# A gated short-convolution layer in fp32: the gate's sums over partitions as two fp32r products, and the output in transfers of 1024 columns

## The chip, the core and the metric

The kernel runs on one core of a Trainium2 chip. The metric is the device time of one execution in microseconds. The engines are TensorE (PE: matmuls, with its weight loads shown as PEld), VectorE (DVE), ScalarE (ACT), GpSimd (POOL) and SyncE (SP), whose queue issues nearly all transfers here. A transfer runs on the core's DMA engines.

## What is computed

One layer over 256 tokens of width D = 2048, with E = 4096 channels in the mixer, all in fp32. Cut to what the one layer of this case does:

```python
def rmsnorm(x, g):
    y = x * lax.rsqrt(jnp.mean(x * x, axis=-1, keepdims=True) + EPS)
    return y * g

def short_conv_mixer(h, w_in, conv_w, w_out):
    proj = jnp.einsum('bsd,de->bse', h, w_in)          # 2048 -> 4 x 4096
    b_gate, c_gate, v, g = jnp.split(proj, 4, axis=-1)
    u = causal_depthwise_conv(c_gate * v, conv_w)      # width 3
    y = b_gate * u * jax.nn.silu(g)
    return jnp.einsum('bse,ed->bsd', y, w_out)         # 4096 -> 2048

mod = jnp.einsum('bd,df->bf', jax.nn.silu(c), ada_w) + ada_b   # 2048 -> 3 x 2048
shift, scale, gate = jnp.split(mod, 3, axis=-1)
h = rmsnorm(x, norm_g) * (1.0 + scale[:, None, :]) + shift[:, None, :]
x = x + gate[:, None, :] * short_conv_mixer(h, sc_w_in, sc_conv_w, sc_w_out)
out = rmsnorm(x, final_g)
```

## The kernel before

**Exact products.** A fp32 matrix is split into two fp32r parts, `hi` (a cast on ScalarE, L337) and `lo` (the fp32 remainder, a subtraction on VectorE, L338). A product of two matrices is then three fp32r matmuls: hi by hi, hi by lo, lo by hi. The weights are loaded raw from memory in tiles of 128 x 2048 (`raw_s`, `raw`, `raw_o`), by SP's queue, with three buffers each for `raw`, `hi` and `lo`. A `raw` buffer is loaded again when VectorE has made its `lo`; a `hi` buffer is cast again when TensorE has used it. TensorE takes 48 matmuls of 256 columns from each tile of the input projection.

**Stages.** First the norm, the first parts of shift and scale and the features `hT`. Then the input projection in two forms: `parts` (tile `mm_s`, up to about 383 us) goes over two channel groups at a time and over parts of the depth, as the shift and scale for more of the depth become known; its sums are kept in `acc` tiles between parts. Then whole products (`mm_b`, up to about 732 us). Last the output projection (`mm_o`), for the four column groups `dc` of 512 columns and the two halves `t` of the tokens.

**The banks in `parts`.** Three PSUM banks of the tag `mm` take turns. When TensorE has finished one, `keep` drains it, on ScalarE by a copy (L497) or on VectorE by an add into `acc` (L499). The bank's next user may be seeded: ScalarE copies an `acc` into it (L511) before TensorE adds to it. VectorE and ScalarE also do `mixed` here: gating, convolution (L408 to L412) and the split of the result `y` (L417, L418).

**The gate.** `gate` is a vector of 2048, needed on all 128 partitions. It is made in four pieces of 512 columns. `ada_w`'s part for it comes in 32 loads (`at_g`, four buffers of the tag `at`), each used by two steps on VectorE, which multiply by `silu_c` and add into `gacc` (two buffers). After 16 steps `gacc` holds, on each partition, a part of the sum. One fp32 matmul with a matrix of ones sums over the partitions and spreads the sum to all of them (L604), and VectorE adds the bias (L605). The text calls the four pieces gate 0 to gate 3.

**The end.** `po[t]` for the last column group already holds x, and the gate is multiplied into the weights, so `po` is the result before the norm. `gated` squares and sums it on ScalarE (L726), and `finish(t)` takes the root and the reciprocal `fs`, multiplies four column pieces of 512 by `fs`, two on VectorE and two on ScalarE, and sends each piece by a transfer of its own on SP's queue (L685). The first half's `finish` runs while TensorE still does the last products of the second half (`late`).

**Order.** In the first stage the instructions of each engine stand in the order of the program. After it a scheduler orders each engine's queue by priorities and its own estimate of times; `later(GIVE)` puts the gate's steps behind other work by 300 places. Each engine then works through its queue in that order, with semaphores for what it needs of others. Buffers of a tag go to whoever is next when one is free.

Of the kernel before, what the change touches and what calls it, by code (L numbers as in the profile page):

```python
# [13 lines left out]
P = 128  # L14
# [114 lines left out]
def short_conv_layer(ctx: ExitStack, tc: tile.TileContext, x, c, norm_g, ada_w, ada_b, w_in, conv_w, w_out, final_g, out):  # L129
# [95 lines left out]

    ident = const.tile([P, P], F32, tag="ident", name="ident")
    make_identity(nc, ident)
    ones = const.tile([P, P], F32, tag="ones", name="ones")
    nc.vector.memset(ones, 1.0)
    eps_t = const.tile([P, 1], F32, tag="eps", name="eps_t")  # L230
    nc.vector.memset(eps_t, EPS)
# [359 lines left out]
    def gate_sums(dc, j, at3):  # L591
        nc.sync.dma_start(at3, adas[:, j : j + 2, 2, dc * 512 : (dc + 1) * 512])
        if j == 0:
            gacc[0] = adap.tile([P, 512], F32, tag="gv", name="gacc")
        ga = gacc[0]
        for i in range(2):
            s = silu_c[:, j + i : j + i + 1]
            if j + i == 0:
                nc.vector.tensor_scalar_mul(ga, at3[:, i, :], s)
            else:  # L600
                nc.vector.scalar_tensor_tensor(out=ga, in0=at3[:, i, :], scalar=s, in1=ga, op0=ALU.mult, op1=ALU.add)
        if j + 2 == KT:
            ps = psum.tile([P, 512], F32, tag="sm", name="ps_gate", bufs=2)
            nc.tensor.matmul(ps, ones, ga, start=True, stop=True)  # L604
            nc.vector.tensor_tensor(out=gate(dc), in0=ps, in1=gate(dc), op=ALU.add)  # L605

    KP = 8
# [63 lines left out]
    def finish(t):  # L671

        fs = const.tile([P, 1], F32, tag="fs", name="fs", bufs=2)
        nc.scalar.activation(fs, fsq[:, t, 3:4], AF.Sqrt, bias=part_sum[:, t : t + 1])
        nc.vector.reciprocal(fs, fs)
        for c0, n, vector in ((0, 512, True), (512, 512, False), (1536, 512, True), (1024, 512, False)):
            dd = slice(c0, c0 + n)
            r = big[:, t, dd]
            if c0 == 1536:
                nc.vector.scalar_tensor_tensor(out=r, in0=po[t], scalar=fs, in1=fg[:, dd], op0=ALU.mult, op1=ALU.mult)  # L680
            elif vector:
                nc.vector.tensor_scalar_mul(r, r, fs)
            else:
                nc.scalar.activation(r, r, AF.Copy, scale=fs)
            nc.sync.dma_start(out[t * P : (t + 1) * P, dd], r)  # L685

    for dc in range(4):
        dcs = slice(dc * 512, (dc + 1) * 512)

        both = [psum.tile([P, TT, 512], F32, tag="mm", name="mm_o") for _ in range(1 + (dc == 3))]  # L690
        po = [both[-t][:, t] for t in range(TT)]
        n_ep = NCT // EP
        late = []
        if dc == 3:

            for t in range(TT):
                nc.scalar.copy(po[t], big[:, t, dcs])
        for ep in range(n_ep):

            first = dc == 0 and ep == 0  # L700
            raw = wpool.tile([P, SLOT], F32, tag="raw" if first else "lo", name="raw_o", bufs=3)
            nc.sync.dma_start(
                raw.rearrange("p (k f) -> p k f", k=EP),
                w_out[0, ep * EP * P : (ep + 1) * EP * P, dcs].rearrange("(k p) f -> p k f", p=P),
            )
            if dc == 3:

                raw3 = raw.rearrange("p (k f) -> p k f", k=EP)
                nc.vector.tensor_tensor(
                    out=raw3, in0=raw3, in1=gate(dc).unsqueeze(1).to_broadcast([P, EP, 512]), op=ALU.mult  # L710
                )
            hi, lo = split(raw, SLOT, "raw")
            out_mm(po[0], 0, ep, hi, lo)
            if dc == 3 and ep >= n_ep - LATE:
                late.append((ep, hi, lo))
            else:
                out_mm(po[1], 1, ep, hi, lo)

        def gated(t, bank, c0, n):

            cs = slice(dc * 512 + c0, dc * 512 + c0 + n)
            r = big[:, t, cs]
            p0 = (dc % 2) * 1024 + t * 512 + c0
            pr = big[:, 3, p0 : p0 + n]
            if dc == 3:
                nc.scalar.activation(pr, bank, AF.Square, scale=D**-0.5, accum_out=fsq[:, t, dc : dc + 1])  # L726
                return
            nc.vector.tensor_tensor(out=pr, in0=bank, in1=gate(dc)[:, c0 : c0 + n], op=ALU.mult)
            nc.vector.tensor_tensor(out=r, in0=r, in1=pr, op=ALU.add)
            nc.scalar.activation(pr, r, AF.Square, scale=D**-0.5, accum_out=fsq[:, t, dc : dc + 1])  # L730
            nc.vector.tensor_tensor(out=r, in0=r, in1=fg[:, cs], op=ALU.mult)
            if dc == 2:
                ps = part_sum[:, t : t + 1]
                nc.vector.reduce_sum(ps, fsq[:, t, 0:3], axis=mybir.AxisListType.X)
                nc.vector.tensor_scalar_add(ps, ps, EPS)

        gated(0, po[0], 0, 512)
        if dc == 3:
            finish(0)
        for ep, hi, lo in late:  # L740
            out_mm(po[1], 1, ep, hi, lo)
        gated(1, po[1], 0, 512)
    finish(1)


# [22 lines left out]
```

## Time and profile before

| | before |
|---|---|
| median of 3 runs | 916.65 us (916.56 to 916.69) |
| profiled execution | 916.12 us, span 914.3 us |
| granted TensorE clock | 0.997 of full speed |
| TensorE busy | 900.3 us (98%) |
| VectorE busy | 627.2 us (69%) |
| ScalarE busy | 449.7 us (49%) |
| DMA traffic | 227.64 MB, 249 GB/s over the span |

Times in the traces count from the start of the profiled execution's span. A row of the timeline gives start and duration in us, engine, line, operation, tiles and shape, and in brackets how long the engine had been idle before and what ended that. A row of the chain gives start, duration, engine, tile and line, and how many instructions were merged. A row for transfers gives the number, the size of one and the median time from issue to landing in us.

### The profile page before, as it was taken

The numbers are of one execution on the slowest core, as the hardware profiler recorded it, in microseconds if no ns is written. First come the engines' busy times: TensorE is split into PE (matmuls) and PEld (weight loads), VectorE is DVE, ScalarE is ACT, GpSimd is POOL, SyncE is SP. The second block draws the span as 40 slices with busy tenths as digits, with TensorE's granted clock in tenths as the row PEclk, the third lists the DMA queues.
The fourth block names the chain that finished last, engine by engine and source line by source line (L and its number), as shares of the span: only waits on it lengthen the run. The fifth ranks groups of instructions, "written<-read, shape, count | busy, mean of one in ns | idle before, by whom it ended". The sixth has DMA issues, their size and how long they took to land.

```text
span 914.3 us, 16328 instructions
## 1 busy us (share of the span) xinstructions
PE 900.3 (98%) x7111; PEld 866.4 (95%) x7111; DVE 627.2 (69%) x601; ACT 449.7 (49%) x423; POOL 0.7 (0%) x6
## 2 busy tenths in 40 slices
PE   7999999999999999999999999999999999999996
PEld 7899999999999999999999999999999988888885
DVE  4888989999986899985555455545455544555882
ACT  6678876554545745543334443334333333443333
POOL 0000000000000000000000000000000000000000
PEclk9999999999999999999999999999999999999998
DMA  9999999999997569867666666566666496565542
GB/s 302 366 384 377 327 348 357 338 360 328 346 366 270 186 231 328 270 217 229 199 186 188 196 201 200 184 189 195 202 188 196 139 352 205 200 205 188 185 139 92
DMA packets 147367, 227.64 MB, mean 249 GB/s; under 512 B 5424, under 2 KB 103904, under 8 KB 146912
## 3 DMA queue, kind: packets, MB, share of 16 engines
q1 hardware_dynamic: 147056, 226.51, 73.7%
q8 instruction: 55, 0.90, 0.4%
q14 instruction: 16, 0.13, 0.0%
q10 hardware_dynamic: 240, 0.09, 0.0%
HBM read 224.49 MB, written 2.10 MB: 248 GB/s over the span
## 4 chain that ended last, share of the span: by engine, by line
PE 95%; DMA 3%; DVE 1%; ACT 1%; SPq 0%; issue 0%; ACTq 0%; DVEq 0%
PE mm_b L465 38%; PE mm_s L465 37%; PE mm_o L666 6%; PE mm_o L667 6%; PE mm_o L665 6%; DMA raw_s<-in_sc_w_in_dram 1%; DMA at<-in_ada_w_dram 1%; DMA x<-in_x_dram 1%; DVE gv L363 1%; PE ps_gate L604 0%; PE tp_g L454 0%; ACT hi L337 0%; SPq L220 0%; DVE lo L338 0%; PE sum L349 0%; SPq L203 0%
## 5 line engine op out<-in xcount | busy, mean ns | idle before, releaser
L465 PE MATMUL mm_b<-hT,hi 128*128 128x256 f32 x2048 | 348.8, 276 | 0.0
L465 PE MATMUL mm_s<-hT,hi 128*128 128x256 f32 x2048 | 337.0, 277 | 1.6 <-ACT hT L327 1.0
L465 PEld LDWEIGHTS mm_b<-hT,hi 128*128 128x128 f32 x2048 | 308.3, 188 | 0.2 <-issue 0.2
L465 PEld LDWEIGHTS mm_s<-hT,hi 128*128 128x128 f32 x2048 | 299.3, 188 | 2.8 <-ACT hT L327 1.2
L465 PE MATMUL mm_b<-hT,lo 128*128 128x256 f32 x1024 | 282.6, 276 | 0.0
L465 PE MATMUL mm_s<-hT,lo 128*128 128x256 f32 x1024 | 262.1, 276 | 0.0
L338 DVE TENSOR_TENSOR lo<-raw,hi 128x2048 fp32r<-128x2048 f32 x64 | 146.7, 2292 | 128.8 <-ACT hi L337 128.7
L337 ACT CAST hi<-raw 128x2048 fp32r<-128x2048 f32 x64 | 122.4, 1913 | 197.2 <-PE mm_b L465 149.9
L465 PEld LDWEIGHTS mm_b<-hT,lo 128*128 128x128 f32 x1024 | 192.2, 188 | 0.2 <-issue 0.2
L465 PEld LDWEIGHTS mm_s<-hT,lo 128*128 128x128 f32 x1024 | 182.8, 188 | 0.0
L337 ACT CAST hi<-raw_s 128x2048 fp32r<-128x2048 f32 (+1 forms) x64 | 121.4, 1901 | 99.5 <-PE mm_s L465 84.5
L338 DVE TENSOR_TENSOR lo<-raw_s,hi 128x2048 fp32r<-128x2048 f32 (+1 forms) x64 | 145.5, 2273 | 22.5 <-ACT hi L337 21.3
L338 DVE TENSOR_TENSOR lo<-raw_o,hi 128x2048 fp32r<-128x2048 f32 x32 | 73.3, 2291 | 64.5 <-ACT hi L337 64.5
L337 ACT CAST hi<-raw_o 128x2048 fp32r<-128x2048 f32 x32 | 61.0, 1907 | 107.2 <-PE mm_o L667 85.1
L666 PE MATMUL mm_o<-lo,y 128*128 128x512 f32 x256 | 99.7, 391 | 0.0
L665 PE MATMUL mm_o<-hi,y 128*128 128x512 f32 x256 | 99.3, 389 | 0.0
L667 PE MATMUL mm_o<-hi,y 128*128 128x512 f32 x256 | 99.3, 389 | 0.0
L447 DVE SCALAR_TENSOR_TENSOR gv<-at,silu_c,gv 128x512 f32<-128x512 f32 x105 | 78.6, 749 | 2.6 <-DMA at<-in_ada_w_dram 0.8
L666 PEld LDWEIGHTS mm_o<-lo,y 128*128 128x128 f32 x256 | 48.1, 188 | 10.2 <-issue 0.2
L667 PEld LDWEIGHTS mm_o<-hi,y 128*128 128x128 f32 x256 | 48.0, 188 | 10.1 <-issue 0.2
L665 PEld LDWEIGHTS mm_o<-hi,y 128*128 128x128 f32 x256 | 48.0, 188 | 10.0
L497 ACT COPY acc<-mm_s 128x1024 f32<-128x1024 f32 x43 | 43.4, 1018 | 22.2 <-PE mm_s L465 22.0
(102 smaller groups left out, 382.0 us busy)
## 6 DMA issues: line engine op xcount, KB each, us to landing
raw<-in_sc_w_in_dram SPq DMA_DIRECT2D x64, 1024.0 KB, 5.6
raw_s<-in_sc_w_in_dram SPq DMA_DIRECT2D x63, 1024.0 KB, 7.6
raw_o<-in_sc_w_out_dram SPq DMA_DIRECT2D x32, 1024.0 KB, 5.2
at<-in_ada_w_dram SPq DMA_DIRECT2D x114, 256.0 KB, 7.1
at_g<-in_ada_w_dram SPq DMA_DIRECT2D x32, 512.0 KB, 7.5
at<-in_ada_w_dram SPq DMA_DIRECT2D x6, 512.0 KB, 9.0
x<-in_x_dram SPq DMA_DIRECT2D x4, 512.0 KB, 6.7
big<-in_x_dram SPq DMA_DIRECT2D x2, 1024.0 KB, 8.0
```

The costliest lines, as they stand in the source:

```text
L337: nc.scalar.copy(hi[:, :n], raw[:, :n])
L338: nc.vector.tensor_tensor(out=lo[:, :n], in0=raw[:, :n], in1=hi[:, :n].bitcast(F32), op=ALU.subtract)
L363: nc.vector.scalar_tensor_tensor(out=gv0, in0=first_ada[k], scalar=c_k, in1=gv0, op0=ALU.mult, op1=ALU.add)
L447: nc.vector.scalar_tensor_tensor(out=gv, in0=at4[:, i], scalar=c_k, in1=gv, op0=ALU.mult, op1=ALU.add)
L465: mm = last_mm[0] = nc.tensor.matmul(dst, w, h[:, k], start=begins and left, stop=ends, skip_group_check=True)
L497: nc.scalar.copy(acc[ch, q], bank)
L665: nc.tensor.matmul(po, yh, hi[:, o], start=opens, stop=False, skip_group_check=True)
L666: nc.tensor.matmul(po, yh, lo[:, o], start=False, stop=False, skip_group_check=True)
L667: nc.tensor.matmul(po, yl, hi[:, o], start=False, stop=ct == NCT - 1, skip_group_check=True)
```

## The change

Two edits. The gate's `gacc` is split into two fp32r parts in one tile `gate_s` (a buffer of the tag `at`, as the loads `at_g` use), by a cast on ScalarE and a subtraction on VectorE, and two fp32r matmuls with the ones replace the fp32 one. The ones are exact in fp32r. At the end, the squaring moves from `gated` into `finish`, and `finish` sends 1024 columns in one transfer when both of their pieces are done; ScalarE's pieces are written ahead of VectorE's.

```diff
-    ones = const.tile([P, P], F32, tag="ones", name="ones")
+    ones_e = const.tile([P, P], F32R, tag="ones", name="ones")
+    ones = ones_e.bitcast(F32)
...
         if j + 2 == KT:
             ps = psum.tile([P, 512], F32, tag="sm", name="ps_gate", bufs=2)
-            nc.tensor.matmul(ps, ones, ga, start=True, stop=True)
+            parts = adap.tile([P, 2, 512], F32R, tag="at", name="gate_s", bufs=4)
+            nc.scalar.copy(parts[:, 0], ga)
+            nc.vector.tensor_tensor(out=parts[:, 1], in0=ga, in1=parts[:, 0].bitcast(F32), op=ALU.subtract)
+            for i in range(2):
+                nc.tensor.matmul(ps, ones_e, parts[:, i], start=i == 0, stop=i == 1)
             nc.vector.tensor_tensor(out=gate(dc), in0=ps, in1=gate(dc), op=ALU.add)
...
     def finish(t):
         fs = const.tile([P, 1], F32, tag="fs", name="fs", bufs=2)
+        r = big[:, t]
+        pr = big[:, 3, 1024 + t * 512 : 1536 + t * 512]
+        nc.scalar.activation(pr, po[t], AF.Square, scale=D**-0.5, accum_out=fsq[:, t, 3:4])
         nc.scalar.activation(fs, fsq[:, t, 3:4], AF.Sqrt, bias=part_sum[:, t : t + 1])
         nc.vector.reciprocal(fs, fs)
-        for c0, n, vector in ((0, 512, True), (512, 512, False), (1536, 512, True), (1024, 512, False)):
-            dd = slice(c0, c0 + n)
-            r = big[:, t, dd]
-            if c0 == 1536:
-                nc.vector.scalar_tensor_tensor(out=r, in0=po[t], scalar=fs, in1=fg[:, dd], op0=ALU.mult, op1=ALU.mult)
-            elif vector:
-                nc.vector.tensor_scalar_mul(r, r, fs)
-            else:
-                nc.scalar.activation(r, r, AF.Copy, scale=fs)
-            nc.sync.dma_start(out[t * P : (t + 1) * P, dd], r)
+        nc.scalar.activation(r[:, 512:1024], r[:, 512:1024], AF.Copy, scale=fs)
+        nc.vector.tensor_scalar_mul(r[:, 0:512], r[:, 0:512], fs)
+        nc.sync.dma_start(out[t * P : (t + 1) * P, 0:1024], r[:, 0:1024])
+        nc.scalar.activation(r[:, 1024:1536], r[:, 1024:1536], AF.Copy, scale=fs)
+        nc.vector.scalar_tensor_tensor(
+            out=r[:, 1536:D], in0=po[t], scalar=fs, in1=fg[:, 1536:D], op0=ALU.mult, op1=ALU.mult
+        )
+        nc.sync.dma_start(out[t * P : (t + 1) * P, 1024:D], r[:, 1024:D])
```

The edit to the gate also moves instructions between about 250 and 430 us, because the scheduler decides anew. TensorE's order keeps its places: the products of gates 0 and 1 stand next to each other between the same `mm_s` products as before (four rows of one matmul now, two before), those of gate 2 in `mm_b`, those of gate 3 in `mm_o`. Three places of other engines follow; the order has no times in it. In the rows of the change lines are numbered one to five higher (L338 is L339, L499 is L500, L601 is L602).

VectorE, at the tile subtractions (`lo_3495`, `lo_3549`) that stand at 285.06 and 290.50 us in the trace of before. Before:

```order
L338 TENSOR_TENSOR lo_3495<-raw_s_3492,hi_3494 128x2048
L338 TENSOR_TENSOR lo_3549<-raw_s_3546,hi_3548 128x2048
L546 TENSOR_TENSOR acc01_373<-acc01_373,acc02_480 128x512 x2
L499 TENSOR_TENSOR acc12_482<-mm_s_3324,acc12_482 128x1024
L409 SCALAR_TENSOR_TENSOR acc02_480<-acc01_373,cw_128,acc02_480 128x255 x2
```

And in the change:

```order
L339 TENSOR_TENSOR lo_3495<-raw_s_3492,hi_3494 128x2048
L607 TENSOR_TENSOR gate_s_6368<-gacc_5550,gate_s_6368 128x512
L600 TENSOR_SCALAR gacc_6488<-at_g_6486,silu_c_129 128x512
L602 SCALAR_TENSOR_TENSOR gacc_6488<-at_g_6486,silu_c_129,gacc_6488 128x512
L602 SCALAR_TENSOR_TENSOR gacc_6488<-at_g_6601,silu_c_129,gacc_6488 128x512 x2
L339 TENSOR_TENSOR lo_3549<-raw_s_3546,hi_3548 128x2048
L547 TENSOR_TENSOR acc01_373<-acc01_373,acc02_480 128x512 x2
L602 SCALAR_TENSOR_TENSOR gacc_6488<-at_g_6721,silu_c_129,gacc_6488 128x512
L500 TENSOR_TENSOR acc12_482<-mm_s_3324,acc12_482 128x1024
```

The subtraction of gate 1 and the first five steps of gate 2 (`gacc_6488`) now stand here; before, gate 2 began about 30 us later.

VectorE again, from the subtraction of `lo_3773` (307.12 us before) to the add that drains the bank `mm_s_3658` (317.10 us before). Before:

```order
L338 TENSOR_TENSOR lo_3773<-raw_s_3770,hi_3772 128x2048
L499 TENSOR_TENSOR acc13_547<-mm_s_3491,acc13_547 128x1024
L338 TENSOR_TENSOR lo_3832<-raw_s_3829,hi_3831 128x2048
L550 TENSOR_TENSOR acc03_545<-acc03_545,acc00_615 128x512 x2
L499 TENSOR_TENSOR acc10_617<-mm_s_3658,acc10_617 128x1024
```

And in the change:

```order
L339 TENSOR_TENSOR lo_3773<-raw_s_3770,hi_3772 128x2048
L413 SCALAR_TENSOR_TENSOR acc12_482<-acc11_412,cw_128,acc12_482 128x254 x2
L602 SCALAR_TENSOR_TENSOR gacc_6488<-at_g_6952,silu_c_129,gacc_6488 128x512
L413 SCALAR_TENSOR_TENSOR acc12_482<-acc11_412,cw_128,acc12_482 128x254
L500 TENSOR_TENSOR acc13_547<-mm_s_3491,acc13_547 128x1024
L339 TENSOR_TENSOR lo_3832<-raw_s_3829,hi_3831 128x2048
L602 SCALAR_TENSOR_TENSOR gacc_6488<-at_g_6952,silu_c_129,gacc_6488 128x512
L551 TENSOR_TENSOR acc03_545<-acc03_545,acc00_615 128x512 x2
L500 TENSOR_TENSOR acc10_617<-mm_s_3658,acc10_617 128x1024
```

Between `lo_3549` and this last add the change has six steps of gate 2 more than before, the fifth to the tenth; the convolution steps (L413) stood ahead of `lo_3773` before and only change places within the stretch.

SP's queue, at the loads of the weight tiles `raw_s_3937` and `raw_s_3991` (the second was issued at 315.30 us before); the names in brackets are the semaphores that an issue waits for. Before:

```order
L524 DMA raw_s_3883<-in_sc_w_in_dram 128x2x1024 [waits DMAHW5_49,DVE_49]
L524 DMA raw_s_3937<-in_sc_w_in_dram 128x2x1024 [waits DMAHW6_49,DMAHW1_49,DVE_49]
L524 DMA raw_s_3991<-in_sc_w_in_dram 128x2x1024 [waits DMAHW7_49,DVE_49]
L524 DMA raw_s_4045<-in_sc_w_in_dram 128x2x1024 [waits DMAHW3_49,DMAHW0_49,DVE_49]
L592 DMA at_g_6944<-in_ada_w_dram 128x2x512 [waits DVE_49]
```

And in the change:

```order
L525 DMA raw_s_3883<-in_sc_w_in_dram 128x2x1024 [waits DMAHW3_49,DVE_49]
L593 DMA at_g_7066<-in_ada_w_dram 128x2x512 [waits DMAHW5_49,DVE_49]
L525 DMA raw_s_3937<-in_sc_w_in_dram 128x2x1024 [waits DMAHW6_49,DVE_49]
L593 DMA at_g_7186<-in_ada_w_dram 128x2x512 [waits PE_49]
L593 DMA at_g_7301<-in_ada_w_dram 128x2x512 [waits PE_49]
L525 DMA raw_s_3991<-in_sc_w_in_dram 128x2x1024 [waits DMAHW0_49,DVE_49]
```

The last two loads of gate 2 wait for TensorE, which frees the `gate_s` buffers of gates 0 and 1 by its gate products, and `raw_s_3991` stands behind them.

More of the change, by code (lines that the diff above doesn't have):

```diff
@@ L724, in gated @@
             pr = big[:, 3, p0 : p0 + n]
-            if dc == 3:
-                nc.scalar.activation(pr, bank, AF.Square, scale=D**-0.5, accum_out=fsq[:, t, dc : dc + 1])
-                return
             nc.vector.tensor_tensor(out=pr, in0=bank, in1=gate(dc)[:, c0 : c0 + n], op=ALU.mult)
@@ L735, in gated @@
                 nc.vector.tensor_scalar_add(ps, ps, EPS)
-        gated(0, po[0], 0, 512)
         if dc == 3:
             finish(0)
+        else:
+            gated(0, po[0], 0, 512)
         for ep, hi, lo in late:
             out_mm(po[1], 1, ep, hi, lo)
-        gated(1, po[1], 0, 512)
-    finish(1)
+        if dc == 3:
+            finish(1)
+        else:
+            gated(1, po[1], 0, 512)
 _INS = ["x", "c", "norm_g", "ada_w", "ada_b", "sc_w_in", "sc_conv_w", "sc_w_out", "final_g"]
```

## The prediction

> **What bounds the kernel now.** I read the page's head first, then TensorE's waits, then the chain of waits around the four gate sums, then the order of instructions in time at the end.
>
> ```profile
> span 914.3 us, 16328 instructions
> PE 900.3 (98%) x7111; PEld 866.4 (95%) x7111; DVE 627.2 (69%) x601; ACT 449.7 (49%) x423; POOL 0.7 (0%) x6
> PE tp_v L239 <- DMA rows<-in_c_dram: 4.0, 1, 4.0
> 234.13 81.66 PE mm_s L465 x720
> 315.79 1.72 PE ps_gate L604 x4
> 675.01 0.86 PE ps_gate L604 x2
> 753.89 0.86 PE ps_gate L604 x2
> 760.00:850.00 90.00, 90.00 (x399) 74.53 (x398) 47.06 (x30) 35.99 (x27) 0.00 (x0) 1.00 0.58 195
> ```
>
> TensorE is busy 900.3 of 914.3 us. The longest of its waits, the third row, lies in the first microseconds. From 234 us on the chain is TensorE alone, matmul after matmul, and the gate sums stand in it like any other work: whatever they cost there, the end pays. The chain's rows are start, duration and count. In the last row (a stretch, then busy time of TensorE, its weight loads, VectorE, ScalarE, GpSimd, with counts; then clock, DMA share, GB/s) TensorE is full, and it ran there nothing but fp32r products of 512 columns: 90.00 / 399 = 0.2256 us each.
>
> **Part 1, the gate sums on TensorE: -1.64 us.** Four fp32 products leave. Each appears in the trace as two MATMULs, so the chain holds eight: 1.72 + 0.86 + 0.86 = 3.44 us, or 0.43 us each. Eight fp32r products of the same 128x512 shape come: 8 x 0.2256 = 1.80 us. The order puts them where the old ones were. Bounds: the fp32r row is the cheapest that this shape has here, so -1.64 is the most; if the split products still went at the fp32 pace, the gain is 0. I take -1.64, since out products and gate products now have the same types and width.
>
> **Part 2, the splitting: hidden.** It adds four casts on ScalarE and four subtractions on VectorE. The same two shapes are in the trace for `y`:
>
> ```profile
> 325.82 0.62 ACT L417 CAST y<-acc 128x512 fp32r<-128x512 f32 x1 [0.99 <-DVE acc L551]
> 330.31 0.68 DVE L418 TENSOR_TENSOR y<-acc,y 128x512 fp32r<-128x512 f32 x1
> 320.00:350.00 30.00, 30.00 (x267) 30.00 (x266) 29.59 (x31) 14.18 (x11) 0.00 (x0) 1.00 0.76 271
> 282.00:320.00 38.00, 38.00 (x326) 37.04 (x325) 28.76 (x35) 26.22 (x28) 0.00 (x0) 1.00 0.60 198
> 281.90 40.61 SPq L524 DMA_DIRECT2D raw_s<-in_sc_w_in_dram  x8
> 290.50 2.29 DVE L338 TENSOR_TENSOR lo<-raw_s,hi 128x2048 fp32r<-128x2048 f32 x1 [3.15 <-ACT hi L337]
> 310.39 1.23 DVE L499 TENSOR_TENSOR acc<-mm_s,acc 128x1024 f32<-128x1024 f32 x1 [0.97 <-PE mm_s L465]
> 312.98 2.29 DVE L338 TENSOR_TENSOR lo<-raw_s,hi 128x2048 fp32r<-128x2048 f32 x1 [1.37 <-ACT hi L337]
> 315.89 1.29 DVE L550 TENSOR_TENSOR acc<-acc,acc 128x512 f32<-128x512 f32 x2 [0.61 <-ACT acc L497]
> 317.10 1.22 DVE L499 TENSOR_TENSOR acc<-mm_s,acc 128x1024 f32<-128x1024 f32 x1
> 318.83 0.48 DVE L599 TENSOR_SCALAR gacc<-at_g,silu_c 128x512 f32<-128x512 f32 x1
> 323.24 0.75 DVE L601 SCALAR_TENSOR_TENSOR gacc<-at_g,silu_c,gacc 128x512 f32<-128x512 f32 x1
> 323.90 1.28 DVE L418 TENSOR_TENSOR y<-acc,y 128x512 fp32r<-128x512 f32 x2
> 318.36 1.02 ACT L511 COPY mm_s<-acc 128x1024 f32<-128x1024 f32 x1 [0.70 <-DVE acc L499]
> 322.92 1.91 ACT L337 CAST hi<-raw_s 128x2048 fp32r<-128x2048 f32 x1 [1.43 <-PE mm_s L465]
> 315.30 0.37 SPq L524 DMA_DIRECT2D raw_s<-in_sc_w_in_dram  x1
> 328.49 1.92 ACT L337 CAST hi<-raw_s 128x2048 fp32r<-128x2048 f32 x1
> at_g<-in_ada_w_dram SPq DMA_DIRECT2D x32, 512.0 KB, 7.5
> ```
>
> So 4 x 0.62 = 2.5 us on ScalarE, which has room (14.18 of 30 us busy), and 4 x 0.68 = 2.7 us on VectorE, which between 320 and 350 us has almost none (29.59 of 30). Their cover is the lead that VectorE has over TensorE, and the change also spends from that lead by moving work. `gacc` comes free when the second part is taken, no longer when TensorE has used it, so gate 2 accumulates from about 288 us on and not from 318.83.
>
> I follow this to the place where it matters most. The add at 317.10 (L499) drains a PSUM bank; ScalarE then refills that bank (318.36, which waited 0.70 for just this add), and TensorE opens on it when it changes tiles, at 322.92 (the cast in that row waited for TensorE to finish the tile before). In the new order six more `gacc` steps of gate 2 stand between the tile subtraction of 290.50 and this add: 6 x 0.66 to 0.75 = 4.0 to 4.5 us (0.75 is the row's duration; 0.66 is 323.90 minus 323.24, the next start). VectorE's idle time in that stretch takes up 0.97 + 1.37 + 0.61 = 2.95. Ahead of 290.50 one subtraction and four steps go into the idle 3.15 us; they fit (0.6 + 4 x 0.66 = 3.2), but the first two pieces of gate 2 stand on SP behind the weight load of 281.90 and behind the last steps of gate 1, so they are asked for only at about 282 and 283 us, and with the 7.5 us of the last row to land the four steps end near 292.3, 1.8 late; if they land early, 0 late. The add then starts at 317.10 + 4.0 - 2.95 = 318.2 at the earliest and 317.10 + 4.5 - 2.95 + 1.8 = 320.5 at the latest, most likely near 319.3. With the add (1.22) and the refill (1.02) the bank is ready at 320.4 to 322.7, near 321.5. TensorE, with two gate sums saved, asks for it at 322.92 - 0.82 = 322.1. So the lead shrinks from 3.5 us to about 0.6, and between its bounds it is +1.7 to -0.6. I cost the move at nothing, up to 0.6 us at the bound.
>
> `gate_s` also holds one of the four `at` buffers from its cast to its product. SP's queue therefore gets two `at_g` loads that wait for TensorE's gate products, and behind them the next weight load, which went out at 315.30 before. It now goes at about 317, lands by 325 with 7.5 us, and its cast stood at 328.49 before: hidden by 3 us.
>
> **Part 3, the end: +0.2 us.**
>
> ```profile
> 906.93 0.70 ACT big L726 x2
> 908.17 0.72 ACT big L684
> 908.17 1.33 ACT L684 ACTIVATE big<-big,fs 128x512 f32<-128x512 f32 x2 [0.23 <-DVE fs L675]
> 908.17 0.49 DVE L682 TENSOR_SCALAR big<-big,fs 128x512 f32<-128x512 f32 x1
> 908.69 0.33 SPq L685 DMA_DIRECT2D out_dram<-big  x1
> 909.11 0.38 SPq L685 DMA_DIRECT2D out_dram<-big  x1
> 909.59 0.41 SPq L685 DMA_DIRECT2D out_dram<-big  x1
> 910.09 0.41 SPq L685 DMA_DIRECT2D out_dram<-big  x1
> out_dram<-big SPq DMA_DIRECT2D x1, 256.0 KB, 2.3
> out_dram<-big SPq DMA_DIRECT2D x1, 256.0 KB, 3.1
> 908.90:909.50 0.60, 0.00 (x0) 0.00 (x0) 0.42 (x1) 0.60 (x1) 0.00 (x0) 0.72 0.00 0
> 909.70:912.00 2.30, 0.00 (x0) 0.00 (x0) 0.00 (x0) 0.00 (x0) 0.00 (x0) 0.50 1.05 375
> L203 SPq DMA_DIRECT2D x<-in_x_dram x4: 385/420/557, 0.7 to 2.1; - x4
> ```
>
> ScalarE and VectorE do the same instructions in the same order; only the four transfers of each half become two. For the second half the first transfer waited for VectorE's 0.49 us (908.66); now it also needs ScalarE's first piece, 908.17 + 0.72 = 908.89, so it goes 0.23 us later. The last needs ScalarE's second piece, 908.17 + 1.33 = 909.50, and SP is free by then (an issue of rows twice as long took 0.42 us for `x`), so it goes at 909.53 instead of 910.09, 0.56 earlier, with twice the bytes. Which counts? The issues land 2.3 us after 908.69 and 3.1 us after 910.09, so at 910.99 and 913.19, and in this time the DMA engines are full (share 1.05 from 909.7 to 912.0): the bytes set the end, not the issues. Then the end moves with the first byte, +0.23. If the issue alone counted, 909.53 + 3.1 = 912.63, -0.56. I take +0.2, by the share row. The first half has nothing to pay: its transfers are over before the second's begin (share 0.00 from 908.9 to 909.5).
>
> The Trainium skill, "DMA: Bandwidth & Descriptors", section "Anatomy of one DMA — SWDGE (gpsimd) path", fits a transfer by a fixed 2.0 us plus its bytes over 436 GB/s; by that the last 512 KB would land at about 909.53 + 3.2 = 912.7, as the last 256 KB would at 910.09 + 2.6, the end would stay where it is, and the sum would be -1.6. The trace disagrees with it at both ends (2.3 us alone, 3.1 us behind others), so the row decides.
>
> **Sum.** -1.64 + 0 + 0.2 = -1.4 us on the profiled execution of 916.12 us (span 914.3), so 914.7. The runs have a median of 916.65, 0.5 above it; 916.65 - 1.4 = 915.2. That is 0.15%, just inside the 0.2% (1.8 us) that a measurement of this kernel tells from no change.
>
> **The rivals.**
> - The end gains too. If landing follows the issue, or longer rows are written faster than 375 GB/s, the end moves by up to -0.56: 916.65 - 1.64 - 0.56 = 914.4. For it: the last landing takes only 0.8 us longer than the first, though three transfers stand ahead. Against it: the full DMA share. Faster by over 0.2% needs the end to gain 0.2.
> - The bank is late. The add behind gate 2's steps ends after 322.1 minus the refill, and TensorE stands still at the tile change: up to 0.6 us by the bounds, 915.8. It begins to cost when the add starts later than 319.9.
> - The same place, dearer, and slower in the end: if `at_g` loads land late several times over (three more are waited for in that stretch), each delay passes to the add. It eats the whole gain from a start of 321.3 on, and the kernel is slower by over 0.2% if the add starts after 323.1: then about 918.7. Against it: my latest bound is 320.5, and the DMA engines have room there (share 0.60 from 282 to 320 us).
> - The Trainium skill, "TensorE: Matmul & The Clock Gate", section "Architectural detail: the array is 16× 32×32, not 1× 128×128", calls ScalarE and VectorE strict first-in, first-out; that speaks against this change, because neither the add nor the refill can pass a `gacc` step that waits for its load. The trace agrees as far as it goes: the add of 317.10 had its bank from TensorE by 315.8, when the chain turns to the gate sums, and stood behind the pair of 315.89.
> - The change doesn't do what it says: the split products keep the 0.43 us pace. Then 916.65 + 0.2 = 916.9. Against it: the out products of the same types run at 0.2256.
>
> **How the numbers follow.** My forecast, with the end between -0.2 and +0.3, has 0.55 (914.8 to 915.3). The end gains: 0.27 (914.3 to 914.8). The bank late by up to 0.6, or a little more: 0.08 (up to 916.5). Slower there: 0.07. No gain on TensorE: 0.03. Of these the second is faster by over 0.2%, with some 0.03 of the first; the slower case is slower; the rest is the same: 0.30, 0.63, 0.07. The likeliest time is 915.2. The range runs from the end's best bound, 914.3, to 916.6, which takes in the late bank and leaves out the slower cases.
>
> **What would show it.** The chain's gate rows should read about 0.90, 0.45 and 0.45 us instead of 1.72, 0.86 and 0.86; TensorE should have no new wait between 234 us and its last product; the add that was at 317.10 should start between 318 and 320.5, and the refill behind it end before TensorE's tile change. At the end, counted from the reciprocal, the first transfer of the last half should go 0.2 us later, the last 0.5 earlier and land 0.2 later, with DMA share near 1 between. A TensorE wait for ScalarE's refill near 322 us makes the sum wrong upward; a last landing well before 3.9 us after the last issue makes it wrong downward.

## The result: faster, and past the forecast

The changed kernel took 913.75 us, median of seven runs (913.23 to 914.23), against 916.65 for the kernel before, measured beside it (seven runs, 915.52 to 917.79). The ratio is 0.9973, with a 95% interval of 0.9963 to 0.9982. The forecast was 915.2 with a range from 914.3: the time lies below that range.

The profiled execution took 913.47 us, 2.65 less than the one before. The page's head after the change:

```profile
span 911.7 us, 16332 instructions
PE 898.6 (99%) x7111; PEld 866.5 (95%) x7111; DVE 628.8 (69%) x605; ACT 451.7 (50%) x427; POOL 0.7 (0%) x6
```

The four instructions more on VectorE and on ScalarE are the splitting; their busy time grew by 1.6 and 2.0 us, and TensorE's fell by 1.7. The chain of waits (start, duration, count) at the gate sums:

```profile
233.76 81.66 PE mm_s L466 x720
315.41 0.92 PE ps_gate L609 x4
674.07 0.23 PE ps_gate L609
674.42 0.24 PE ps_gate L609
752.33 0.47 PE ps_gate L609 x2
```

0.92 + 0.23 + 0.24 + 0.47 = 1.86 us where 3.44 stood: -1.58. The first row begins 0.37 earlier than before, which is not of the change: the load of `x` at the start took less time, and in the runs below the same sums begin anywhere between 314.72 and 316.45 (314.74 in e2, whose code up to there is that of the kernel before). The longest waits of TensorE still lie at the start of the kernel; between 234 us and the last product the view, which lists waits over 0.15 us, has none:

```profile
PE tp_v L240 <- DMA rows<-in_c_dram: 4.2, 1, 4.2
PE mm_s L466 <- ACT hi L338: 1.0, 1, 1.0
```

The order in time around the bank that the prediction followed, VectorE's add (L500), ScalarE's refill (L512) and the cast at the tile change (L338), and SP's loads:

```profile
318.18 1.23 DVE L500 TENSOR_TENSOR acc<-mm_s,acc 128x1024 f32<-128x1024 f32 x1
319.44 1.02 ACT L512 COPY mm_s<-acc 128x1024 f32<-128x1024 f32 x1 [1.76 <-DVE acc L500]
321.75 1.92 ACT L338 CAST hi<-raw_s 128x2048 fp32r<-128x2048 f32 x1 [0.17 <-PE mm_s L466]
315.90 1.07 SPq L593 DMA_DIRECT2D at_g<-in_ada_w_dram  x2
317.08 0.40 SPq L525 DMA_DIRECT2D raw_s<-in_sc_w_in_dram  x1
```

The add starts 1.1 us later than before and the refill ends at 320.46, 1.3 us ahead of the tile change at 321.75: the lead shrank from 3.5 us and still hides the splitting.

The rest of the gain is at the end. The order in time of the last half before the change began with this reciprocal (the rows behind it stand in the prediction):

```profile
907.97 0.16 DVE L675 RECIPROCAL fs<-fs 128x1 f32<-128x1 f32 x1 [2.36 <-ACT fs L674]
```

From its end at 908.13 to the end of the span there were 6.19 us. (The expectations below give 6.17 and 5.52 for the two ends, read from rounded rows.) After the change:

```profile
906.02 0.16 DVE L683 RECIPROCAL fs<-fs 128x1 f32<-128x1 f32 x1 [2.36 <-ACT fs L682]
906.21 0.72 ACT L684 ACTIVATE big<-big,fs 128x512 f32<-128x512 f32 x1 [0.23 <-DVE fs L683]
906.84 0.71 ACT L687 ACTIVATE big<-big,fs 128x512 f32<-128x512 f32 x1
906.96 0.33 SPq L686 DMA_DIRECT2D out_dram<-big  x1
907.58 0.33 SPq L691 DMA_DIRECT2D out_dram<-big  x1
```

From 906.18 to the end of the span there are 5.50 us: -0.69, where +0.2 was forecast. The gate's -1.58 and this -0.69 make -2.27; the other 0.4 of the profiled execution's 2.65 is the start told above.

Three views show where the 0.69 comes from. First the two stretches from the first to the last packet of the last half's 1 MB, before and then after (columns as in the prediction: the last two are DMA share and GB/s):

```profile
909.51:912.65 3.14, 0.00 (x0) 0.00 (x0) 0.00 (x0) 0.00 (x0) 0.00 (x0) 0.50 0.93 334
```

```profile
907.79:910.44 2.65, 0.00 (x0) 0.00 (x0) 0.00 (x0) 0.00 (x0) 0.00 (x0) 0.87 0.97 396
```

The same bytes take about 0.48 us less (2.65 instead of 3.13; the first stretch is rounded outward), at nearly the same share of busy DMA engines. Then the kernel's last line, with SP's semaphore waits and its drain (count, ns of one, first and last start; the last two of the eight belong to the steps behind the drain), before and after:

```profile
L764 SPq EVENT_SEMAPHORE  x8: 17/28/28, 913.2 to 914.3; - x8
L764 SPq DRAIN  x3: 7/7/7, 913.6 to 913.9; - x3
```

```profile
L770 SPq EVENT_SEMAPHORE  x8: 17/28/28, 908.0 to 911.6; - x8
L770 SPq DRAIN  x3: 7/7/7, 910.9 to 911.2; - x3
```

The program gives its transfers eight semaphores in turn, and SP at the end waits for them in a fixed order, in six instructions ahead of the drain. Before, the last transfer was on the one that is waited for first, so all six, about 0.06 us each, ran after the last landing at 913.2. Four transfers less in the kernel move the last one to a later place: the first wait is over at 908.0, and only the last two end after the landing.

This table is worked out from the records of packets, semaphores and instructions in the traces, for the second half of the tokens; times in us from the end of the last reciprocal. "Packets" is first to last packet, "signal" is from the last packet to the last of the 16 semaphore increments (the landing), "waits" from there to SP's drain; from the drain to the end it is 0.74 to 0.75 in all.

| kernel | transfers, row | first and last issue | first packet | packets | signal | landing | waits | end |
|---|---|---|---|---|---|---|---|---|
| before | 4, 2 KB | 0.55, 1.95 | 1.38 | 3.13 | 0.55 | 5.06 | 0.39 | 6.19 |
| after | 2, 4 KB | 0.78, 1.40 | 1.61 | 2.65 | 0.35 | 4.61 | 0.14 | 5.50 |
| e1, gate only | 4, 2 KB | 0.55, 1.95 | 1.38 | 3.12 | 0.57 | 5.08 | 0.38 | 6.20 |
| e2, output only | 2, 4 KB | 0.78, 1.39 | 1.62 | 2.64 | 0.36 | 4.61 | 0.14 | 5.50 |
| e6 | 2, 2 KB | 0.78, 1.42 | 1.98 | 2.72 | 0.39 | 5.08 | 0.14 | 5.97 |
| e3 | 4, 2 KB | 0.55, 1.95 | 1.38 | 3.14 | 0.63 | 5.15 | 0.38 | 6.28 |
| e7 | 4, 2 KB, two queues | 0.55, 1.45 | 1.38 | 3.03 | 0.57 | 4.98 | 0.39 | 6.11 |
| e5 | 1, 8 KB | 1.40, 1.40 | 2.26 | 2.60 | 0.38 | 5.24 | 0.27 | 6.25 |
| e8 | 3, 2 and 4 KB | 0.55, 1.46 | 1.38 | 3.01 | 0.49 | 4.88 | 0.25 | 5.88 |
| e9 | 2, 4 KB | 0.78, 1.39 | 1.62 | 2.64 | 0.36 | 4.62 | 0.38 | 5.75 |
| e10 | 2, 3 and 5 KB | 0.59, 1.40 | 1.43 | 2.63 | 0.35 | 4.41 | 0.14 | 5.30 |

The first half of the tokens, which does not end the kernel, repeats the difference in packets: 3.05 us before and 2.64 after.

### The profile page after: what moved, and what is told of

It is laid out like the page before. It is cut to its first block, busy times and chain, and to the rows that moved or that the text cites. A ratio compares the mean times of both kernels' runs of the same rounds, so it can differ in the third digit from the quotient of the medians.

```text
span 911.7 us, 16332 instructions
## 1 busy us (share of the span) xinstructions
PE 898.6 (99%) x7111; PEld 866.5 (95%) x7111; DVE 628.8 (69%) x605; ACT 451.7 (50%) x427; POOL 0.7 (0%) x6
## 4 chain that ended last, share of the span: by engine, by line
PE 95%; DMA 3%; DVE 1%; ACT 0%; SPq 0%; issue 0%; ACTq 0%; DVEq 0%
PE mm_b L466 38%; PE mm_s L466 37%; PE mm_o L671 6%; PE mm_o L670 6%; PE mm_o L672 6%; DMA raw_s<-in_sc_w_in_dram 1%; DMA at<-in_ada_w_dram 1%; DMA x<-in_x_dram 1%; DVE gv L364 1%; PE tp_g L455 0%; ACT hi L338 0%; PE ps_gate L609 0%; SPq L220 0%; DVE lo L339 0%; PE sum L350 0%; SPq L203 0%
## 5 line engine op out<-in xcount | busy, mean ns | idle before, releaser
L339 DVE TENSOR_TENSOR lo<-raw,hi 128x2048 fp32r<-128x2048 f32 x64 | 146.7, 2291 | 128.2 <-ACT hi L338 128.2
L338 ACT CAST hi<-raw 128x2048 fp32r<-128x2048 f32 x64 | 122.5, 1913 | 196.3 <-PE mm_b L466 149.0
L338 ACT CAST hi<-raw_s 128x2048 fp32r<-128x2048 f32 (+1 forms) x64 | 121.4, 1901 | 96.6 <-PE mm_s L466 79.5
L339 DVE TENSOR_TENSOR lo<-raw_s,hi 128x2048 fp32r<-128x2048 f32 (+1 forms) x64 | 145.4, 2272 | 21.2 <-ACT hi L338 20.1
L339 DVE TENSOR_TENSOR lo<-raw_o,hi 128x2048 fp32r<-128x2048 f32 x32 | 73.3, 2290 | 64.0 <-ACT hi L338 64.0
L338 ACT CAST hi<-raw_o 128x2048 fp32r<-128x2048 f32 x32 | 61.0, 1907 | 106.7 <-PE mm_o L672 81.3
```

Source lines behind the costliest of these rows:

```text
L338: nc.scalar.copy(hi[:, :n], raw[:, :n])
L339: nc.vector.tensor_tensor(out=lo[:, :n], in0=raw[:, :n], in1=hi[:, :n].bitcast(F32), op=ALU.subtract)
```

## The experiments

The kernels ran in three sets (e1, e2, e0, e4; then e6, e3, e7, e5; then e9, e8, e10), each with the kernel before on the same chip: 916.15 us (30 runs), 916.26 (28) and 916.28 (21). Medians of the kernels scatter by some tenths of a microsecond, so what concerns the end is read from the traces, whose ends repeat within 0.02 us.

**e1, the gate's edit alone.** The output code is that of the kernel before (cut; all diffs below are against the changed kernel):

```diff
-        nc.sync.dma_start(out[t * P : (t + 1) * P, 0:1024], r[:, 0:1024])
...
+        for c0, n, vector in ((0, 512, True), (512, 512, False), (1536, 512, True), (1024, 512, False)):
...
+            nc.sync.dma_start(out[t * P : (t + 1) * P, dd], r)
```

> Only the gate's products are changed; the output goes as before, in four transfers of 512 columns for each half. If the time went 1.6 us at the gate and 0.65 at the end, as the two profiles say, this run gains the 1.6 alone: the gate rows of the chain about 0.92 + 0.46 + 0.46 = 1.84 instead of 3.44, the stretch from the last reciprocal to the end of the span as before (6.16 us), a median 1.6 us (0.17%) below before. The rival, that the new order on VectorE and ScalarE brings more than the products, says over 2.3 us below before.

914.91 us (11 runs), 0.9985 of before (0.9976 to 0.9993). The chain and SP's last issues:

```profile
315.13 0.92 PE ps_gate L609 x4
906.45 1.81 SPq L690 DMA_DIRECT2D out_dram<-big  x4
```

The gate sums shrink as in the changed kernel, and the end is that of the kernel before, 6.20 us. So -1.58 is the gate's.

**e2, the output's edit alone.** The gate sums are the old fp32 products:

```diff
-            parts = adap.tile([P, 2, 512], F32R, tag="at", name="gate_s", bufs=4)
-            nc.scalar.copy(parts[:, 0], ga)
-            nc.vector.tensor_tensor(out=parts[:, 1], in0=ga, in1=parts[:, 0].bitcast(F32), op=ALU.subtract)
-            for i in range(2):
-                nc.tensor.matmul(ps, ones_e, parts[:, i], start=i == 0, stop=i == 1)
+            nc.tensor.matmul(ps, ones, ga, start=True, stop=True)
```

> Only the end is changed; the gate's sums stay fp32 products and the order up to the output stays that of before. If the end gains by itself, the stretch from the last reciprocal to the end of the span is 5.5 us instead of 6.16, and the median lies 0.65 us (0.07%) below before. My prediction's reading (the bytes set the end, from the first byte on) says 6.4 us and 0.2 us above before.

915.39 us, 0.9991 (0.9982 to 1.0). The chain and the last issues:

```profile
314.74 1.72 PE ps_gate L604 x4
907.86 0.33 SPq L681 DMA_DIRECT2D out_dram<-big  x1
908.48 0.33 SPq L686 DMA_DIRECT2D out_dram<-big  x1
```

The gate rows are the old ones and the end is 5.50 us. The output part is faster by 0.69 alone, with no help from the gate; the interval of the runs reaches 1, so this rests on the trace.

**e0, both parts again**, in the same set.

> The changed kernel once more, beside its parts on the same chip. If the parts add up, it lies 2.2 us (0.25%) below before; the last tenths that its first profile had beyond that (0.37 us, by the landing of the first loads of x) are not of the change and need not come again.

913.50 us, 0.9972 (0.9962 to 0.9982), end 5.50. By the medians of this set the gate gave -1.24, the output -0.76 and both -2.65; by the profiles -1.58, -0.69 and -2.27. Within the scatter of the medians the parts add.

**e4, four transfers with the long rows.** Each transfer of 1024 columns is cut into two of 64 rows:

```diff
-        nc.sync.dma_start(out[t * P : (t + 1) * P, 0:1024], r[:, 0:1024])
+        for h in (0, 64):
+            nc.sync.dma_start(out[t * P + h : t * P + h + 64, 0:1024], r[h : h + 64, 0:1024])
...
```

> The changed kernel, but each transfer of 1024 columns is cut by rows: two transfers of 64 rows x 1024 columns. So four transfers of 256 KB for each half, as before the change, but with rows of 4 KB as after it, all issued when both pieces are done. If the longer rows make the data go faster, the data phase of the last half stays near 2.5 us and the stretch from the last reciprocal to the end of the span stays at 5.5 to 5.7. If the number of transfers or the time of the last issue makes it (issues 0.4 to 0.5 us apart, the last one about 2.0 us after the reciprocal as before, instead of 1.4), the stretch is 6.0 to 6.3 us again.

916.15 us, 1.0002 (0.9993 to 1.0011), and an end of 7.8 us. The issues themselves took 0.47 to 1.00 us, so the last went 2.84 us after the reciprocal and not at about 2.0. Over the stretch of the last half's transfers the rate is not that of any other kernel here:

```profile
907.90:913.00 5.10, 0.00 (x0) 0.00 (x0) 0.00 (x0) 0.00 (x0) 0.00 (x0) 0.75 0.74 253
```

It was meant to tell the number of transfers from the length of rows, and doesn't: transfers over 64 partitions bring a slowness of their own (253 GB/s where 396 stood). The first half is slow too and lands 2.94 us after the last reciprocal, so about 0.24 MB of its data were written in this stretch as well. The run is inconclusive for its question.

**e6, two transfers with the short rows.** Each transfer takes two pieces that do not lie side by side, so its rows are 2 KB; ScalarE does its two pieces in the other order:

```diff
-        nc.sync.dma_start(out[t * P : (t + 1) * P, 0:1024], r[:, 0:1024])
+        oq = out[t * P : (t + 1) * P, :].rearrange("p (a b f) -> p a b f", a=2, b=2)
+        rq = r.rearrange("p (a b f) -> p a b f", a=2, b=2)
+        nc.sync.dma_start(oq[:, :, 0, :], rq[:, :, 0, :])
...
+        nc.sync.dma_start(oq[:, :, 1, :], rq[:, :, 1, :])
```

> The changed kernel, but each of the two transfers of a half takes two pieces that do not lie side by side: columns 0:512 with 1024:1536, then 512:1024 with 1536:2048. Number, size and times of the issues stay those of the changed kernel (first about 0.78 us after the last reciprocal, last about 1.4), but a row of a transfer is 2 KB again, as before the change, and there are twice as many rows. Counted from the end of the last reciprocal to the end of the span (6.17 before the change, 5.52 after it): if the longer rows made the gain, the bytes take 3.1 us again instead of 2.5, the bandwidth falls off at the end as it did before, and the end is 6.0 to 6.2. If the earlier last issue or the smaller number of transfers made it, it stays 5.5.

914.08 us, 0.9975 (0.9965 to 0.9986). The end went to 5.97 us, which the row-length theory had forecast, but not for its reason. The two issues in the order of time, and the stretch of the packets:

```profile
907.67 0.53 SPq L688 DMA_DIRECT2D out_dram<-big  x1
908.31 0.56 SPq L693 DMA_DIRECT2D out_dram<-big  x1
```

```profile
908.85:911.60 2.75, 0.00 (x0) 0.00 (x0) 0.00 (x0) 0.00 (x0) 0.00 (x0) 0.50 0.98 381
```

The bandwidth does not fall: the packets take 2.72 us, nearly the 2.65 of the long rows. What moved the end is the start: an issue of 256 rows takes 0.53 us instead of 0.33, and its first packet comes 1.19 us after it, not 0.83. So short rows cost 0.36 us here through the issue and 0.07 through the rate; not the rows but the cut into four transfers makes the 3.13. (Number and size go together, since the 1 MB is fixed: four transfers are 256 KB each.)

**e3, four transfers in the new order of work.**

```diff
-        nc.sync.dma_start(out[t * P : (t + 1) * P, 0:1024], r[:, 0:1024])
+        for c in (0, 512):
+            nc.sync.dma_start(out[t * P : (t + 1) * P, c : c + 512], r[:, c : c + 512])
...
-        nc.sync.dma_start(out[t * P : (t + 1) * P, 1024:D], r[:, 1024:D])
+        for c in (1024, 1536):
+            nc.sync.dma_start(out[t * P : (t + 1) * P, c : c + 512], r[:, c : c + 512])
```

> The changed kernel, but four transfers of 512 columns for each half, issued in two pairs when both pieces of a pair are done. First issue as in the changed kernel (0.78 us after the last reciprocal), last about 2.0 instead of 1.4, rows of 2 KB. From the reciprocal to the end of the span: if the number of issues or the time of the last one sets the end, 6.1 to 6.4; if the row length does, 6.0 to 6.2 as well; if only the order of the last pieces mattered, 5.5. The order of the semaphores at the end is that of the kernel before, with the last transfer on the one that is waited for first: if that costs, 1.1 us lie between the last landing and the end of the span, else 0.8.

914.41 us, 0.9977 (0.9968 to 0.9987). My expectation of the first issue was wrong: each transfer waits only for its own piece, so the first goes at 0.55. The stretch of the packets:

```profile
907.13:910.27 3.14, 0.00 (x0) 0.00 (x0) 0.00 (x0) 0.00 (x0) 0.00 (x0) 0.81 0.95 334
```

Packets 3.14 us, signal 0.63, waits 0.38, end 6.28. It is the old end again: the rest of the output's edit, without the fewer transfers, gained nothing.

**e7, four transfers on two queues**, so that the last is issued as early as in the changed kernel:

```diff
-        nc.sync.dma_start(out[t * P : (t + 1) * P, 0:1024], r[:, 0:1024])
+        nc.sync.dma_start(out[t * P : (t + 1) * P, 0:512], r[:, 0:512])
+        nc.sync.dma_start(out[t * P : (t + 1) * P, 512:1024], r[:, 512:1024])
...
-        nc.sync.dma_start(out[t * P : (t + 1) * P, 1024:D], r[:, 1024:D])
+        nc.scalar.dma_start(out[t * P : (t + 1) * P, 1024:1536], r[:, 1024:1536])
+        nc.sync.dma_start(out[t * P : (t + 1) * P, 1536:2048], r[:, 1536:2048])
```

> The changed kernel, but four transfers of 512 columns for each half, each issued as soon as its piece is done: columns 0:512, 512:1024 and 1536:2048 by SP, 1024:1536 by ScalarE's own queue. The first issue comes 0.55 us after the last reciprocal and the last about 1.5, with rows of 2 KB. From the reciprocal to the end of the span: if the time of the last issue sets the end, 5.5 to 5.6; if the row length does, 3.1 us for the bytes from a first byte 0.2 earlier, 5.8 to 6.1; if it is the number of transfers on one queue, below 5.5.

914.66 us, 0.9976 (0.9965 to 0.9986), end 6.11. The last issue and the packets:

```profile
908.66 0.41 SPq L693 DMA_DIRECT2D out_dram<-big  x1
```

```profile
908.59:911.63 3.04, 0.00 (x0) 0.00 (x0) 0.00 (x0) 0.00 (x0) 0.00 (x0) 0.74 0.95 345
```

The first issue is 0.23 earlier than in the changed kernel and the last only 0.05 later, and still the landing comes 0.37 later than in the changed kernel. The last issue does not set the end, and a second queue does not take away what four transfers cost.

**e5, one transfer for each half**, when all four pieces are done:

```diff
-        nc.sync.dma_start(out[t * P : (t + 1) * P, 0:1024], r[:, 0:1024])
-        nc.sync.dma_start(out[t * P : (t + 1) * P, 1024:D], r[:, 1024:D])
+        nc.sync.dma_start(out[t * P : (t + 1) * P, :], r)
```

> The changed kernel, but one transfer of 2048 columns (1 MB, rows of 8 KB) for each half, issued when all four pieces are done, about 1.5 us after the last reciprocal. If the bytes set the end from the first byte on, the first byte is 0.7 later and the end is 5.52 + 0.7 = 6.2. If the last issue sets it, as it does not move by more than 0.1, the end is 5.5 to 5.6. If still longer rows gain again (0.6 us from 2 KB to 4 KB), 5.6 to 6.0.

914.28 us, 0.9978 (0.9968 to 0.9989), end 6.25. The issue, at the time of the changed kernel's last, and the packets:

```profile
908.17 0.36 SPq L690 DMA_DIRECT2D out_dram<-big  x1
```

```profile
909.03:911.65 2.62, 0.00 (x0) 0.00 (x0) 0.00 (x0) 0.00 (x0) 0.00 (x0) 0.50 0.95 400
```

Rows of 8 KB and a single transfer gain 0.05 us in the packets; the first issue is 0.61 later and the landing 0.62. Where the packets take about as long, with one transfer or two, the first byte does set the end.

**e9, the order of the last waits.** The half that ends the kernel is unchanged; the half before it goes out in six transfers, which moves the last transfer back to the first-waited semaphore:

```diff
-        nc.sync.dma_start(out[t * P : (t + 1) * P, 0:1024], r[:, 0:1024])
+        cuts = (0, 1024) if t else (0, 384, 768, 1024)
+        for a, b in zip(cuts, cuts[1:]):
+            nc.sync.dma_start(out[t * P : (t + 1) * P, a:b], r[:, a:b])
...
```

> The changed kernel, but the first half of the tokens goes out in six transfers instead of two (three of the first 1024 columns, three of the rest). The second half, which ends the kernel, is as in the changed kernel: two transfers, issued 0.78 and 1.4 us after the last reciprocal. What the four more transfers ahead of it do is to move the last transfer on to the semaphore on which the last one of the kernel before stood, which SP waits for first at the end, so that five waits stand behind it and not one. If the order of these waits is worth 0.24 us of the gain, the last landing stays 4.6 us after the reciprocal and the end of the span goes from 5.5 to 5.75. If it is worth nothing, the end stays 5.5. If the first half's transfers do disturb the end, the landing moves too.

914.25 us, 0.9977 (0.9968 to 0.9986). The last line's waits and drain on SP:

```profile
L774 SPq EVENT_SEMAPHORE  x8: 17/28/28, 910.1 to 911.2; - x8
L774 SPq DRAIN  x3: 7/7/7, 910.5 to 910.8; - x3
```

The landing stays (4.62), the waits take 0.38 again and the end is 5.75: 0.24 us of the change's gain is the place of one semaphore in a list.

**e8, three transfers.**

```diff
-        nc.sync.dma_start(out[t * P : (t + 1) * P, 0:1024], r[:, 0:1024])
+        nc.sync.dma_start(out[t * P : (t + 1) * P, 0:512], r[:, 0:512])
+        nc.sync.dma_start(out[t * P : (t + 1) * P, 512:1024], r[:, 512:1024])
```

> The changed kernel, but the first 1024 columns of each half go in two transfers of 512 again, so three transfers in all: the first issue comes 0.55 us after the reciprocal instead of 0.78, the last stays at 1.4. If the first byte and the bytes set the end and the number of transfers costs nothing, the last landing comes 0.24 earlier, at 4.4. If each transfer beyond two costs what the traces so far show (four cost 0.49 us of data time and 0.2 us of the last signal more than two do, so one some 0.3), it comes at 4.6 to 4.8, no better than now. The wait order costs up to 0.2 more: end of the span 5.2 to 5.3 by the first, 5.6 to 5.8 by the second.

914.21 us, 0.9981 (0.9972 to 0.999), end 5.88. The stretch of the packets:

```profile
907.18:910.20 3.02, 0.00 (x0) 0.00 (x0) 0.00 (x0) 0.00 (x0) 0.00 (x0) 0.95 0.92 347
```

The first packet comes 0.23 earlier, the packets take 3.01 us and the landing is at 4.88, dearer than both my figures: the third transfer costs nearly as much as two more do.

**e10, a better cut**: two transfers, at column 768:

```diff
-        nc.scalar.activation(r[:, 512:1024], r[:, 512:1024], AF.Copy, scale=fs)
+        nc.scalar.activation(r[:, 512:768], r[:, 512:768], AF.Copy, scale=fs)
...
-        nc.sync.dma_start(out[t * P : (t + 1) * P, 0:1024], r[:, 0:1024])
-        nc.scalar.activation(r[:, 1024:1536], r[:, 1024:1536], AF.Copy, scale=fs)
+        nc.sync.dma_start(out[t * P : (t + 1) * P, 0:768], r[:, 0:768])
+        nc.scalar.activation(r[:, 768:1536], r[:, 768:1536], AF.Copy, scale=fs)
...
-        nc.sync.dma_start(out[t * P : (t + 1) * P, 1024:D], r[:, 1024:D])
+        nc.sync.dma_start(out[t * P : (t + 1) * P, 768:D], r[:, 768:D])
```

> A version meant to be better than both: two transfers for each half as in the changed kernel, but cut at column 768 instead of 1024. ScalarE's first piece is then 256 columns (about 0.45 us) and its second 768 (about 1.0), so the first transfer waits for VectorE's 0.49 us only and goes 0.55 us after the reciprocal instead of 0.78, and the last at about 1.4 as now. If the first byte and the rate of two transfers set the end, the last landing comes 0.2 to 0.25 earlier (4.35 to 4.4 instead of 4.6), the end of the span 5.25 to 5.3 instead of 5.5, and the time is 0.2 us below the changed kernel, which the runs can hardly tell. If the last issue set the end, it stays 5.5.

913.43 us, 0.997 (0.9958 to 0.9981). ScalarE's two pieces and the two issues:

```profile
906.67 0.51 ACT L684 ACTIVATE big<-big,fs 128x256 f32<-128x256 f32 x1 [0.23 <-DVE fs L683]
907.09 0.92 ACT L687 ACTIVATE big<-big,fs 128x768 f32<-128x768 f32 x1
907.23 0.33 SPq L686 DMA_DIRECT2D out_dram<-big  x1
908.04 0.33 SPq L691 DMA_DIRECT2D out_dram<-big  x1
```

The first issue is 0.19 earlier, the last where it was, the landing at 4.41 and the end at 5.30: 0.20 less than the changed kernel, as the first byte has it. The runs can't tell 913.43 from 913.50, but the trace can.

## Why the prediction was wrong, point by point

**Part 1 was right.** -1.64 forecast, -1.58 measured. Each product now takes about 0.233 us in the chain and not 0.2256.

**Part 2 was right in its mechanism, and at the early edge of its bounds.** The add was to start between 318.2 and 320.5, most likely near 319.3, and started at 318.18: the loads of gate 2 came early, so its first four steps ended at 290.8 and not near 292.3; the weight load behind `at_g` was to go at about 317 and went at 317.08; there is no new wait of TensorE. The late-bank rivals did not occur. That the lead is what hides it stays true: 1.3 us are left of 3.5, where 0.6 was the likeliest forecast.

**Part 3 failed**, and with it the sum: +0.2 forecast, -0.69 measured. The issues moved as forecast (first +0.23, last -0.55). "The bytes set the end, not the issues. Then the end moves with the first byte, +0.23" was half right: e5 and e10 show that the end follows the first byte, and the first packet did come 0.23 later. What failed was the unsaid half, that the same bytes take the same time, and that what lies behind the last packet stays: the prediction put these terms at nothing without a reason. Its own sign of being wrong showed: the last landing came 3.2 us after the last issue, not 3.9. By the table:

| term | before | after | difference |
|---|---|---|---|
| first packet | 1.38 | 1.61 | +0.23 |
| packets | 3.13 | 2.65 | -0.48 |
| signal | 0.55 | 0.35 | -0.20 |
| waits at the end | 0.39 | 0.14 | -0.24 |
| sum | | | -0.69 |

The first row's term was the forecast; the other three had none. The share row of the prediction (1.05, 375 GB/s) showed busy engines, but a busy engine is not an engine at its pace. The packet records show it: a packet of 2048 B takes 84 ns in most cases, but of the 512 packets of the last half before the change 55 took over 1.2 times that, up to 193 ns, and the engines did not end together. In the changed kernel, e6 and e10 there is not one such packet. Per engine the packets of the half add up to 2.88 us before the change and 2.69 in e6, which has the same rows: the slow packets are 0.19 of the 0.41 us between these two, and the rest is time in which some engines had no packet. e6 shows that it is not the rows, e7 that it is neither the time of the last issue nor the single queue, e8 that it begins with the third transfer: before the change and in e3, e7 and e8 the first slow packet starts 2.35 to 2.36 us after the reciprocal, 0.9 to 1.0 us after the third transfer's issue. The count alone is not the cause: in e9's first half, six transfers of 128 and 192 KB, 8 of 768 packets were slow, though the packets took 3.06 us there too (the last issue came only 2.92 us after that half's reciprocal). Why packets slow down when three or four transfers of 256 KB or more are under way is not shown by these runs.

**The rival "the end gains too"** had the sign and 0.27 of the chance, but both of its mechanisms fall: landing does not follow the last issue (in e5 and e10 the last issue stays at 1.40 and the landing moves by +0.62 and -0.20), and long rows are written faster by 0.07 us only (e6). That the landing itself moved by -0.45, near this rival's figure, is chance: it is the sum of the first three rows of the table. The rival also stopped at -0.56, since it had no term behind the landing.

**The Trainium skill** fits a transfer by 2.0 us and its bytes over 436 GB/s ("DMA: Bandwidth & Descriptors", section "Anatomy of one DMA — SWDGE (gpsimd) path"); the fit is for transfers issued from GpSimd, and these go from SP. By it my estimate had the last 512 KB land 3.2 us after their issue; they took 3.22. The first 512 KB took 2.61, though, and the 1 MB of e5 3.84, where estimates by the fit are 3.2 and 4.4, so the hit is chance. The same page's section "Why a DMA increments its semaphore by 16 and not by 1" says that each engine signals for itself, after its own data. The traces agree: the 16 increments of the last transfer are spread over 0.70 us before the change and 0.15 after it, and the landing is the last of them. Why that last increment comes 0.55 us after the last packet before the change, and 0.35 after it, is not shown.

**The base.** I took 916.65 for the kernel before, a median of three. The seven runs beside the result have the same median, but over the 79 runs of the later sets it is 916.2, and 916.2 - 2.27 = 913.9, beside 913.75 and 913.50 measured. Of the 1.45 us between forecast and result 0.9 is Part 3; about 0.4 is the base, if the later sets are taken for it. By its median the change is faster by 0.3%, to which the prediction gave 0.30 of the chance (over 0.2%); the interval, 0.18 to 0.37%, reaches just below that line.

## What to carry to other kernels

Follow the last transfer to the last instruction of the span, with a term each for first packet, packets, signal and the waits behind the landing; a DMA share near 1 doesn't say that the engines run at their pace, the GB/s beside it does. For the last megabyte two transfers beat one, three and four here, and a cut at which the first can go as soon as VectorE's piece is done (e10) gained 0.20 us more. Differences of 0.2 us at the end of a kernel are below what its runs can tell, and still plain in the trace.

## What the runs showed of the hardware

- Packets of the output, SBUF to DRAM, took 84 ns for 2 KB, 121 for 3 KB, 159 for 4 KB, 196 for 5 KB and 309 for 8 KB (medians): about 9 ns and 27 bytes per ns on each engine. With long rows and two transfers the 16 engines wrote at 396 GB/s.
- Two transfers over 64 partitions each were much slower than one over 128 (e4): 253 GB/s, with packets of 4 KB that took up to 446 ns instead of 159 to 166, and issues of 0.47 to 1.00 us on SP.
- In the last half an issue of 128 rows took SP 0.33 us where the half went in two transfers, 0.36 where it went in one, and 0.38 to 0.41 from the second on where it went in three or four; one of 256 rows took 0.53 to 0.56. The first packet came 0.83 to 0.86 us after the start of an issue of 128 rows, 1.19 after one of 256.
- SP's waits at the end of the program take about 0.06 us each even when their semaphores have long been reached.
